# Expert weights of one decoder layer loaded as 2 MB units for a pair of experts, in nine buffers

## The chip, the cores and the metric

One core of one Trainium2 chip runs the whole program. The metric is the device time of one execution in microseconds (us); smaller is better. The engines are TensorE (PE in the profile: matrix products; PEld its weight loads), VectorE (DVE), ScalarE (ACT), GpSimd (POOL) and SyncE (SP), which issues most transfers. SBUF is the memory on the chip with 128 rows (partitions), PSUM the accumulators of TensorE. Transfers between HBM and SBUF run on 16 DMA engines.

## The reference, cut to what matters

One inference step of one decoder layer on 576 tokens (512 of a prompt, 64 of samples), model width 1024: a mixer (gated linear attention and dilated attention side by side), cross attention, and a mixture of experts; then a last norm. The change lies in the mixture of experts. Each token is sent to one of 4 groups and to 2 of the 8 experts in it, 32 experts in all. All arithmetic is in float32.

```python
def expert_block(a):
    xb, e = a
    return (jax.nn.silu(xb @ w_e1[e]) * (xb @ w_e3[e])) @ w_e2[e]
...
y = jax.ops.segment_sum(yb.astype(jnp.float32) * row_w[:, None], row_tok, num_segments=N + 1)[:N]
```

`w_e1` and `w_e3` are 1024 x 512 for each expert, `w_e2` is 512 x 1024: 6 MB an expert, 192 MB in all, each byte read once.

## The kernel before

Up to about 596 us the kernel computes the mixer, the cross attention and the routing. What follows is the expert loop at L1568, one turn for a **pair** of experts, p = 0 to 15; four pairs make one group of experts. Each expert has 64 places for tokens, so that a pair fills 128 rows.

One turn: `scales` (L1519, L1522) turns the routing weights of the pair. The **first products** at L1575 multiply the pair's tokens (tile `X`) by w_e1 and w_e3 (side by side, `w13`): for k = 0 to 7, column block c = 0, 1 (w_e1, w_e3) and expert e = 0, 1, each with 512 columns; the profile counts 64 instructions for a pair, since each float32 product is two. ScalarE's silu (L1597) and VectorE's product (L1600) make `sg`, four transposes follow (L1603), and the **second products** at L1616 multiply by w_e2 in two column blocks of 512 (32 instructions in the profile). `split_tile` (L243, L244) splits the result into two parts `yhi` and `ylo`, and `combine` (L1535 on TensorE, L1537 on VectorE) adds them to the rows of the group in `acc`. The combining of pair p runs in turn p + 1, half of it behind the first products, half behind the transposes. Where a group ends, `finish` norms its rows and stores them (L1367); meanwhile the next group's rows are fetched, split and gathered (`fetch_group`, `split_group`, `gather`, L1501 to L1509). In turn 9 `general` (L1448 on) looks on every engine whether some expert had more than 64 tokens; here none has, and the branch is not taken. In the last turn the second products go in four blocks of 256 columns, and `last_norm` (L1547 to L1558) norms the last rows behind them; POOL scales the first CUT = 128 columns there (L1556), ScalarE the next 384 (L1557), VectorE the rest (L1558).

**The weights.** `_lay_out` stores `w13` as 32 x 4 pieces and `w2` as 32 x 2 pieces, each 128 rows of 8 KB. One piece is one transfer of 1 MB, 12 for a pair (8 of w13, 4 of w2), 192 in all, each issued from SP by `load_one` (L1313 for w13, L1321 for w2). The last pair's w2 is the exception: its four 1 MB buffers hold one block of 256 columns of both experts, filled by two transfers each whose rows are in pieces of 1 KB (L1328). The buffers are a ring of 18 (`HOMES`): 13 in the pool `wpa`, which is there early, and 5 in `wpb`, whose space is free only when the routing is done. `loads_to` at the end of each turn lets the loads run 18 buffers ahead. What orders them on the chip: a transfer waits on SP for its buffer to be released by TensorE, and for its lane; SP has eight lanes for transfers, and so has at most eight in flight. Transfers 16 to 18 wait also for the first fetch of token rows (`i_first`, L1206), so that these come first. The rows of two groups lie in one tile `acc` of 128 x 4 x 1024 numbers, which the routing uses as scratch before.

Of the kernel before, what the change touches and what calls it, by code (L numbers as in the profile page):

```python
# [21 lines left out]
T = 576  # L22
NP_ = 512
D = 1024
# [3 lines left out]
CHUNK_A, CHUNK_B = 13, 5  # L28
PAY = 24
GENERAL = 9  # L30
CUT = 128
# [67 lines left out]
def _lay_out(inputs):  # L99
# [76 lines left out]
def body(ctx: ExitStack, tc: tile.TileContext, I, O, dbg=None):  # L176
# [847 lines left out]
    acc = keep.tile([128, 4, D], F32, name="acc")  # L1024
# [57 lines left out]
    with ExitStack() as st:  # L1082
        rp = pool(st, "route")
        space = acc.rearrange("p a c -> p (a c)")
        acc3, last = space[:, 0:T], space[:, T:2 * T]
        gp.memset(space[:, 2 * T:2048], 0.0)
        gp.memset(space[64:128, 3584:4096], 0.0)
        stage = [space[:, 2048 + i * 512:2560 + i * 512].rearrange("p (i c) -> p i c", c=128) for i in range(3)]
        stage4 = space[0:64, 3584:4096]
        hots = [space[:, a:a + 320].bitcast(BF16).rearrange("p (i c) -> p i c", c=128) for a in (2048, 3072)]  # L1090
# [115 lines left out]
        i_first = [fetch_rows(acc[:, t], src[:, t:t + 1]) for t in range(2)][-1]  # L1206
# [19 lines left out]
        posm = rt(5, 32)  # L1226
# [67 lines left out]
    def hp_():  # L1294
# [3 lines left out]
    HOMES = [(wpa, f"wa{i}") for i in range(CHUNK_A)] + [  # L1298
        (wpb, f"wb{i}") for i in range(CHUNK_B)]
# [3 lines left out]
    def wchunk():  # L1303
        home, tag = HOMES[len(ring) % RING]
        ring.append(home.tile([128, 2048], F32, name=f"wc{len(ring)}", tag=tag))
        return ring[-1]

    def load_one(p, n):

        w = wchunk()  # L1310
        if n < 8:
            q, h = divmod(n, 2)
            i_w = sy.dma_start(w, I["w13"][2 * p + h, q])  # L1313
            if CHUNK_A + 2 < len(ring) <= RING:
                tc.add_manual_dep(i_w.ins, i_first.ins.name, mybir.DependencyInfo(
                    mybir.DependencyClass.Sync, mybir.DependencyReason.DATA), reason="the first rows before more weights")
# [16 lines left out]
    def loads_to(n):  # L1333
        for i in range(len(ring), min(n, 192)):
            load_one(*divmod(i, 12))
# [228 lines left out]
    for p in range(16):  # L1564
        if p == 0:
            gather(0, oh, X, range(4))
# [77 lines left out]
```

## Time and profile before

| | us |
|---|---|
| median of three runs | 1080.32 (1078.32 to 1082.83) |
| profiled execution | 1076.97 |
| its span | 1075.3 |
| TensorE busy | 1019.0 (95%) |
| VectorE busy | 456.6 (42%) |
| ScalarE busy | 340.6 (32%) |
| POOL busy | 62.3 (6%) |

The span runs from the first to the last instruction of the profiled execution; the execution's own time has 1.67 us around it. Busy shares are means over the span: TensorE and the DMA engines are each full in different parts of it. The mean granted clock of TensorE was 0.978 of full speed. HBM reads were 290.30 MB.

### The profile page before, as it was taken

Reading aid. Unit: us, or ns where it says so; the run is one execution under the profiler, and the core shown is the slowest. Engines: PE = TensorE matmul, PEld = TensorE weight load, DVE = VectorE, ACT = ScalarE, POOL = GpSimd, SP = SyncE. Lnnn points to the kernel's source line nnn. Section 1 sums busy time; section 2 is a strip of 40 time slices with the busy share of each in tenths; the row PEclk is TensorE's granted clock in tenths of the full one; section 3 lists DMA queues with packets and bytes.
Section 4 is the critical chain, followed back from the end, with each engine's and each line's share of the span. In section 5 each row is a group of like instructions: output and inputs, shape, how many; then the busy total and the mean of one; then the engine's idle time right before and its main releaser. Section 6 shows DMA issues by size and latency. Waiting matters only on the chain. (4 is left out here: it accounts for less than half of the span.)

```text
span 1075.3 us, 17989 instructions
## 1 busy us (share of the span) xinstructions
PE 1019.0 (95%) x7375; PEld 711.8 (66%) x7375; DVE 456.6 (42%) x1043; ACT 340.6 (32%) x695; POOL 62.3 (6%) x87
## 2 busy tenths in 40 slices
PE   8999999999999999999997899999899969999996
PEld 7998889886779999888996444354435334443333
DVE  6337875357645764455333425223322322222113
ACT  5355323267444633333231111113211311122103
POOL 2100010000000200000111000001000100001002
PEclk9999999999999999999998799999999989999999
DMA  7312016517875752666693799999999999999993
GB/s 258 119 40 79 27 60 235 213 46 249 323 281 194 265 185 88 215 212 213 248 374 125 294 420 421 421 421 421 420 421 421 421 417 421 421 421 420 421 404 122
DMA packets 59674, 300.46 MB, mean 279 GB/s; under 512 B 7288, under 2 KB 13929, under 8 KB 35136
## 3 DMA queue, kind: packets, MB, share of 16 engines
q1 hardware_dynamic: 53856, 282.66, 67.7%
q0 software_dynamic: 5120, 16.28, 4.1%
q8 instruction: 59, 0.97, 0.4%
q10 hardware_dynamic: 608, 0.30, 0.1%
q14 instruction: 31, 0.25, 0.1%
HBM read 290.30 MB, written 12.19 MB: 281 GB/s over the span
## 5 line engine op out<-in xcount | busy, mean ns | idle before, releaser
L1575 PE MATMUL hp<-wc,X 128*64 128x512 f32 x1024 | 241.7, 595 | 6.3 <-DMA wc<-w 6.3
L1575 PEld LDWEIGHTS hp<-wc,X 128*64 128x64 f32 x1024 | 88.4, 137 | 151.5 <-issue 131.3
L283 PE MATMUL pj<-hi,whi 128*128 128x288 f32 (+1 forms) x544 | 163.0, 301 | 0.5 <-ACT R1t L193 0.5
L283 PE MATMUL pj<-hi,wlo 128*128 128x288 f32 (+1 forms) x544 | 162.4, 299 | 0.0
L283 PE MATMUL pj<-lo,whi 128*128 128x288 f32 (+1 forms) x544 | 162.1, 298 | 0.0
L1616 PE MATMUL hp<-wc,sg 128*64 128x512 f32 (+1 forms) x544 | 121.8, 575 | 0.1
L234 ACT ACTIVATE whi<-wst 128x1024 fp32r<-128x1024 f32 (+1 forms) x62 | 65.6, 1059 | 148.8 <-PE pj L283 121.1
L283 PEld LDWEIGHTS pj<-hi,whi 128*128 128x128 f32 x544 | 103.3, 190 | 4.2 <-issue 2.6
L283 PEld LDWEIGHTS pj<-hi,wlo 128*128 128x128 f32 x544 | 103.4, 190 | 1.7 <-issue 1.4
L283 PEld LDWEIGHTS pj<-lo,whi 128*128 128x128 f32 x544 | 103.4, 190 | 1.3 <-issue 0.8
L235 DVE TENSOR_TENSOR wlo<-wst,whi 128x1024 fp32r<-128x1024 f32 (+1 forms) x62 | 76.0, 1226 | 44.8 <-ACT whi L234 44.8
L1616 PEld LDWEIGHTS hp<-wc,sg 128*64 128x64 f32 x544 | 39.0, 138 | 69.9 <-issue 64.7
L1600 DVE SCALAR_TENSOR_TENSOR sg<-hp,sv,sg 128x512 f32<-128x512 f32 x16 | 12.0, 750 | 171.4 <-PE hp L1575 158.5
L1597 ACT ACTIVATE sg<-hp,sv 128x512 f32<-128x512 f32 x16 | 11.0, 687 | 195.7 <-PE hp L1575 195.7
L1537 DVE TENSOR_TENSOR acc<-acc,cp 128x512 f32<-128x512 f32 (+1 forms) x66 | 42.5, 667 | 61.7 <-PE cp L1535 61.2
L244 DVE TENSOR_TENSOR ylo<-hp,yhi 128x512 fp32r<-128x512 f32 (+1 forms) x34 | 22.4, 659 | 73.3 <-ACT yhi L243 71.4
L308 PE MATMUL pj<-whi,hi 128*128 128x256 f32 (+1 forms) x184 | 53.1, 288 | 0.0
L308 PE MATMUL pj<-wlo,hi 128*128 128x256 f32 (+1 forms) x184 | 52.8, 287 | 0.0
L308 PE MATMUL pj<-whi,lo 128*128 128x256 f32 (+1 forms) x184 | 52.5, 286 | 0.0
L243 ACT ACTIVATE yhi<-hp 128x512 fp32r<-128x512 f32 (+1 forms) x34 | 19.4, 571 | 83.8 <-PE hp L1616 82.0
L1501 PE MATMUL xp<-oh,pthi 128*128 128x256 f32 x128 | 34.7, 305 | 8.9 <-DVEq L1449 7.0
L283 PE MATMUL pj<-h1lo,whi 128*128 128x288 f32 x128 | 38.8, 303 | 0.0
(441 smaller groups left out, 1644.3 us busy)
## 6 DMA issues: line engine op xcount, KB each, us to landing
wc<-w SPq DMA_DIRECT2D x188, 1024.0 KB, 19.8
kv<-kc SPq DMA_DIRECT2D x16, 768.0 KB, 6.9
kv<-vc SPq DMA_DIRECT2D x16, 768.0 KB, 4.8
ckv<-mkc SPq DMA_DIRECT2D x16, 512.0 KB, 6.0
ckv<-mvc SPq DMA_DIRECT2D x16, 512.0 KB, 5.0
wst<-w_qkb SPq DMA_DIRECT2D x8, 512.0 KB, 3.6
wst<-w_mk SPq DMA_DIRECT2D x8, 512.0 KB, 5.6
wst<-w_mv SPq DMA_DIRECT2D x8, 512.0 KB, 4.5
```

Of the source, the lines that this page charges most:

```text
L234: ac.activation(hi[:, s], w[:, s], AF.Copy)
L235: ve.tensor_tensor(lo[:, s], w[:, s], hi[:, s].bitcast(F32), op=OP.subtract)
L243: ins = ac.activation(hi, x, AF.Copy)
L244: ve.tensor_tensor(lo, x, hi.bitcast(F32), op=OP.subtract)
L283: pe.matmul(p, lhsT=a[:, k], rhs=b[k][:, c], start=(k == 0 and s == 0), stop=(k == KT - 1 and s == 2))
L308: pe.matmul(outs[i][0:m], lhsT=a[xk][:, i * 128:i * 128 + m], rhs=b[:, k, :], start=(kh == 0 and k == 0 and s == 0 and head), stop=(kh == ...
L1501: pe.matmul(ps[:, k * 256:k * 256 + 256], lhsT=pt[s][:, c, kk * 128:kk * 128 + 128], rhs=oh[:, c], start=(k + c + s == 0), stop=(k + c + s ...
L1537: ve.tensor_tensor(a, a, ps, op=OP.add)
L1575: i_h = pe.matmul(H[c][rows[e]], lhsT=X[:, k, at + e * 64:at + e * 64 + 64], rhs=views[p, "in", k // 2, e](k % 2, c), start=(k == 0), stop ...
L1597: ac.activation(sg, H[0], AF.Silu, scale=sv[:, 0:1])
L1600: ve.scalar_tensor_tensor(sg, H[1], sv[:, 1:2], sg, op0=OP.mult, op1=OP.mult)
L1616: i_y = pe.matmul(Y[rows[e]], lhsT=hT_[:, j, rows[e]], rhs=views[p, "out", c, e](j), start=(j == 0), stop=(j == 3))
```

## The change

- **Layout.** `w13` and `w2` are stored by pair: a unit is 128 rows of 16 KB, of which the first 8 KB are the first expert's and the rest the second's. A unit is 2 MB and one transfer (L1329); a pair has six, four of w13 and two of w2, 96 in all.
- **Buffers.** The ring has nine homes of 2 MB instead of 18 of 1 MB, in the same space: six in `wpa`, one split home with a half in each pool, two in `wpb`. A unit in the split home comes as two transfers of 1 MB with 8 KB rows (L1332). With eight lanes up to 16 MB can now be in flight.
- **One-time buffers.** Pair 0's first unit goes not into the ring but into `w_first`, which lies in the second place of the rows' tile (not used until the second group's rows are fetched), and `wsecond`, which lies in one of the two places of `X`. `first_loads` issues these in an order of its own.
- **Rows.** `acc` becomes two turning tiles of 128 x 2 x 1024 (`group_rows`); the routing's scratch moves accordingly, and two memsets on POOL go.
- **The last pairs.** The loads end in the order w13 of pair 14, w13 of 15, w2 of 14, w2 of 15. The first products of pair 15 are issued ahead of the transposes and second products of pair 14. Pair 15's w2 has an array of its own, `w2l`: four transfers of 1 MB with 8 KB rows (L1335). The combining of pair 14 stands behind the first block of 256 columns of pair 15.
- **Last norm.** POOL's part of the scaling goes; ScalarE scales 512 columns.
- `general` and `dense`, for the case of too many tokens, read the new layout by pair and half.

```diff
-CHUNK_A, CHUNK_B = 13, 5
+UNITS_A, UNITS_B = 6, 2
...
-CUT = 128
...
-    w13 = np.concatenate([f["w_e1"][0], f["w_e3"][0]], 2).reshape(32, 4, 2, 128, 1024)
-    a["w13"] = ca(w13.transpose(0, 1, 3, 2, 4)).reshape(32, 4, 128, 2048)
-    w2 = f["w_e2"][0].reshape(32, 4, 128, 2, 512)
-    a["w2"] = ca(w2.transpose(0, 3, 2, 1, 4)).reshape(32, 2, 128, 2048)
+    w13 = np.concatenate([f["w_e1"][0], f["w_e3"][0]], 2).reshape(16, 2, 4, 2, 128, 1024)
+    a["w13"] = ca(w13.transpose(0, 2, 4, 1, 3, 5)).reshape(16, 4, 128, 4096)
+    w2 = f["w_e2"][0].reshape(16, 2, 4, 128, 2, 512)
+    a["w2"] = ca(w2.transpose(0, 4, 3, 1, 2, 5)).reshape(16, 2, 128, 4096)
+    a["w2l"] = ca(a["w2"][15].reshape(2, 128, 2, 4, 2, 256).transpose(0, 4, 1, 2, 3, 5)).reshape(4, 128, 2048)
...
-    acc = keep.tile([128, 4, D], F32, name="acc")
+    def group_rows():
+        return keep.tile([128, 2, D], F32, name="acc", bufs=2)
+    w_first = keep.tile([128, 2048], F32, name="wfirst", tag="acc", bufs=2)
+    accs = [group_rows()]
...
-    HOMES = [(wpa, f"wa{i}") for i in range(CHUNK_A)] + [
-        (wpb, f"wb{i}") for i in range(CHUNK_B)]
+    HOMES = [(wpa, f"wa{i}") for i in range(UNITS_A)] + [None] + [(wpb, f"wb{i}") for i in range(UNITS_B)]
     RING = len(HOMES)
     ring, views = [], {}
-    def wchunk():
-        home, tag = HOMES[len(ring) % RING]
-        ring.append(home.tile([128, 2048], F32, name=f"wc{len(ring)}", tag=tag))
+    def whome():
+        i = len(ring)
+        home = HOMES[i % RING]
+        if home:
+            w = home[0].tile([128, 4096], F32, name=f"wc{i}", tag=home[1])
+            ring.append([w[:, 0:2048], w[:, 2048:4096], w])
+        else:
+            ring.append([x.tile([128, 2048], F32, name=f"wh{i}", tag=t) for x, t in ((wpa, "wah"), (wpb, "wbh"))] + [None])
         return ring[-1]
-    def load_one(p, n):
-        w = wchunk()
-        if n < 8:
-            q, h = divmod(n, 2)
-            i_w = sy.dma_start(w, I["w13"][2 * p + h, q])
-            if CHUNK_A + 2 < len(ring) <= RING:
-                tc.add_manual_dep(i_w.ins, i_first.ins.name, mybir.DependencyInfo(
-                    mybir.DependencyClass.Sync, mybir.DependencyReason.DATA), reason="the first rows before more weights")
-            w = w.rearrange("p (k c) -> p k c", k=2)
-            views[p, "in", q, h] = lambda k2, c: w[:, k2, c * 512:c * 512 + 512]
-        elif p < 15:
-            c, h = divmod(n - 8, 2)
-            sy.dma_start(w, I["w2"][2 * p + h, c])
-            w = w.rearrange("p (j c) -> p j c", j=4)
-            views[p, "out", c, h] = lambda j: w[:, j]
+    order = [(p, n) for p in range(14) for n in range(6)] + [(p, n) for ns in (range(4), range(4, 6)) for p in (14, 15)
+                                                             for n in ns]
+    def load(i, w, halves=(0, 1)):
+        p, n = order[i]
+        if n < 4 or p < 15:
+            x = I["w13"][p, n] if n < 4 else I["w2"][p, n - 4]
+            if w[2] is not None:
+                out = sy.dma_start(w[2], x)
+            else:
+                for h in halves:
+                    out = sy.dma_start(w[h], x[:, h * 2048:h * 2048 + 2048])
         else:
-            c = n - 8
-            w = w.rearrange("p (h j c) -> p h j c", h=2, j=4)
             for h in range(2):
-                sy.dma_start(w[:, h], I["w2"][2 * p + h, c // 2].rearrange("p (j c) -> p j c", j=4)[
-                    :, :, c % 2 * 256:c % 2 * 256 + 256])
-            views[p, "out", c, 0] = lambda j: w[:, 0, j]
-            views[p, "out", c, 1] = lambda j: w[:, 1, j]
+                out = sy.dma_start(w[h], I["w2l"][2 * (n - 4) + h])
+        for h in range(2):
+            if n < 4:
+                views[p, "in", n, h] = lambda k2, c, v=w[h].rearrange("p (k c) -> p k c", k=2): v[:, k2, c * 512:c * 512 + 512]
+            elif p < 15:
+                views[p, "out", n - 4, h] = lambda j, v=w[h].rearrange("p (j c) -> p j c", j=4): v[:, j]
+            else:
+                for e in range(2):
+                    views[p, "out", 2 * (n - 4) + h, e] = lambda j, v=w[h].rearrange(
+                        "p (h j c) -> p h j c", h=2, j=4)[:, e]: v[:, j]
+        return out
+    loaded = [0]
     def loads_to(n):
-        for i in range(len(ring), min(n, 192)):
-            load_one(*divmod(i, 12))
+        n = min(n, len(order))
+        for i in range(loaded[0], n):
+            load(i, whome())
+        loaded[0] = max(loaded[0], n)
+    def first_loads():
+        first = [w_first, mw.tile([128, 2048], F32, name="wsecond", tag="X", bufs=2), None]
+        load(0, first, (0,))
+        for i in range(1, UNITS_A + 1):
+            load(i, whome())
+        split = whome()
+        load(UNITS_A + 1, split, (0,))
+        load(0, first, (1,))
+        load(UNITS_A + 1, split, (1,))
+        for i in range(UNITS_A + 2, RING + 1):
+            ins = load(i, whome())
+            tc.add_manual_dep(ins.ins, i_first.ins.name, mybir.DependencyInfo(
+                mybir.DependencyClass.Sync, mybir.DependencyReason.DATA), reason="the first rows before more weights")
+        loaded[0] = RING + 1
...
-            gp.tensor_scalar(a[:, 0:CUT], a[:, 0:CUT], r, None, op0=OP.mult)
-            ac.activation(a[:, CUT:512], a[:, CUT:512], AF.Copy, scale=r)
+            ac.activation(a[:, 0:512], a[:, 0:512], AF.Copy, scale=r)
...
+        sg = gated(p, H, sv)
+        if p == 14:
+            loads_to(len(order))
+            with tc.issue_after(i_h.ins):
+                so15 = scales(15, oh)
+                H15, i_h = first_products(15, X)
+        ps = turned(sg)
...
+    sv, oT = so15
+    sg = gated(15, H15, sv)
+    ps = turned(sg)
+    ac.activation(sg, ps, AF.Copy)
+    sgT = sg.rearrange("p (a b) -> p a b", a=4)
+    y = outputs(15)
+    for c in range(4):
+        i_y = second_products(15, c, 256, sgT, y)
+        with tc.issue_after(i_y.ins):
+            if c == 0:
+                combine(*done, slice(0, D))
+            elif c == 1:
+                combine(y, oT, 15, slice(0, 512), last_norm)
+            elif c == 3:
+                combine(y, oT, 15, slice(512, 768), last_norm)
+                combine(y, oT, 15, slice(768, D), last_norm)
```

How the instructions stand now, at three places. On SP, where the first weights are issued (wc are the ring's buffers, wst belongs to a projection ahead of the experts; the numbers count tiles), before:

```order
L1313 DMA wc_6719<-w 128x2048
L1313 DMA wc_6721<-w 128x2048
L1321 DMA wc_6723<-w 128x2048
L1321 DMA wc_6725<-w 128x2048
L1321 DMA wc_6727<-w 128x2048
L1321 DMA wc_6729<-w 128x2048
L1313 DMA wc_6731<-w 128x2048
L1313 DMA wc_6733<-w 128x2048
L1313 DMA wc_6735<-w 128x2048
L1313 DMA wc_6737<-w 128x2048
L1313 DMA wc_6739<-w 128x2048
L1313 DMA wc_6741<-w 128x2048
```

and after, where wfirst, wsecond and the halves wh of the split home stand among the ring's:

```order
L1332 DMA wfirst<-w 128x2048
L1329 DMA wc_6711<-w 128x4096
L229 DMA wst<-w_co 128x1024 x2
L1329 DMA wc_6713<-w 128x4096
L1329 DMA wc_6715<-w 128x4096
L1329 DMA wc_6717<-w 128x4096
L1329 DMA wc_6719<-w 128x4096
L1332 DMA wh_6721<-w 128x2048
L1332 DMA wh_6722<-w 128x2048
L1329 DMA wc_6726<-w 128x4096
L1332 DMA wsecond<-w 128x2048
L1329 DMA wc_6728<-w 128x4096
```

Before, 18 transfers of 1 MB are issued ahead of the first that waits for a release by the experts' products (wc_6963, the next of these on SP); the last three wait for the fetch of rows. After, wc_6709 (one wst ahead of wfirst) and these eleven, 20 MB in all, are; wc_6726 is the first that waits for the fetch, wsecond stands behind it, and wc_6951, the next on SP, waits for a release.

On TensorE, the end of the program, from the transposes of the last pair on, before:

```order
L1603 MATMUL xp<-ident,sg 128x128 x4
L1535 MATMUL cp<-yhi,oT 128x512
L1535 MATMUL cp<-ylo,oT 128x512
L1616 MATMUL hp<-wc_11188,sg 64x256
L1535 MATMUL cp<-yhi,oT 128x512
L1535 MATMUL cp<-ylo,oT 128x512
L1616 MATMUL hp<-wc_11188,sg 64x256 x7
L1616 MATMUL hp<-wc_11191,sg 64x256 x8
L1616 MATMUL hp<-wc_11194,sg 64x256
L1535 MATMUL cp<-yhi,oT 128x512 x2
L1535 MATMUL cp<-ylo,oT 128x512 x2
L1616 MATMUL hp<-wc_11194,sg 64x256 x7
```

and after, from the last two units of first products on:

```order
L1606 MATMUL hp<-wc_12003,X 64x512 x8
L1606 MATMUL hp<-wc_12005,X 64x512 x8
L1622 MATMUL xp<-ident,sg 128x128 x4
L1635 MATMUL hp<-wc_12007,sg 64x512 x8
L1635 MATMUL hp<-wc_12072,sg 64x512 x8
L1635 MATMUL hp<-wc_12074,sg 64x256 x8
L1570 MATMUL cp<-yhi,oT 128x512
L1570 MATMUL cp<-ylo,oT 128x512
L1570 MATMUL cp<-yhi,oT 128x512
L1570 MATMUL cp<-ylo,oT 128x512
L1635 MATMUL hp<-wc_12074,sg 64x256 x3
L1570 MATMUL cp<-yhi,oT 128x512
```

Before, the four blocks of pair 15 follow its own first products. After, its first products (wc_12005 is their last unit) stand ahead of pair 14's second products (wc_12007 and wc_12072), and its own blocks (wc_12074, and behind these rows wc_12077) come last; the combining of pair 14 (L1570) stands between its first two blocks.

On SP, the last weights, before:

```order
L1313 DMA wc_11087<-w 128x2048
L1313 DMA wc_11089<-w 128x2048
L1313 DMA wc_11184<-w 128x2048
L1313 DMA wc_11186<-w 128x2048
L1328 DMA wc_11188<-w 128x4x256 x2
L1328 DMA wc_11191<-w 128x4x256 x2
L1328 DMA wc_11194<-w 128x4x256 x2
L1328 DMA wc_11197<-w 128x4x256 x2
```

and after:

```order
L1329 DMA wc_12001<-w 128x4096
L1329 DMA wc_12003<-w 128x4096
L1329 DMA wc_12005<-w 128x4096
L1329 DMA wc_12007<-w 128x4096
L1329 DMA wc_12072<-w 128x4096
L1335 DMA wc_12074<-w2l 128x2048 x2
L1335 DMA wc_12077<-w2l 128x2048 x2
```

The eight transfers of 1 KB pieces (128x4x256) become four of whole rows from `w2l`, and the last w13 unit moves ahead of the w2 of pair 14.

## Rows read from the trace of the kernel before

**Rows 1.** the page's busy tenths in 40 slices of the span, and GB/s

```profile
PE   8999999999999999999997899999899969999996
DMA  7312016517875752666693799999999999999993
GB/s 258 119 40 79 27 60 235 213 46 249 323 281 194 265 185 88 215 212 213 248 374 125 294 420 421 421 421 421 420 421 421 421 417 421 421 421 420 421 404 122
```

**Rows 2.** the chain of waits, its longest pieces: start, us, what

```profile
907.15 19.81 DMA wc<-w
...
1027.70 19.95 DMA wc<-w
1047.69 3.65 PE hp L1575 x12
```

**Rows 3.** the waits: engine and line, for what: us, times, longest

```profile
SPq L1313 <- DMA wc<-w: 183.4, 87, 3.4
...
PEld hp L1575 <- DMA wc<-w: 17.2, 20, 2.2
```

**Rows 4.** windows: length, busy by engine (count), PEclk, DMA share, GB/s

```profile
272.00:280.00 8.00, 8.00 (x116) 5.99 (x104) 4.41 (x12) 3.80 (x9) 0.00 (x0) 1.00 1.02 421
464.00:468.00 4.00, 3.88 (x21) 3.13 (x20) 1.78 (x4) 1.34 (x5) 0.00 (x0) 1.00 1.01 412
640.00:860.00 220.00, 214.56 (x1050) 95.50 (x1048) 64.51 (x148) 44.69 (x87) 7.40 (x7) 0.99 1.01 421
884.00:1040.00 156.00, 151.60 (x710) 66.37 (x709) 35.99 (x67) 29.34 (x56) 2.82 (x2) 1.00 1.01 421
1045.00:1050.00 5.00, 4.34 (x17) 1.45 (x16) 0.00 (x0) 0.00 (x0) 0.00 (x0) 1.00 0.99 331
```

**Rows 5.** DMA issues of the page whose rows are 6 and 4 KB

```profile
kv<-kc SPq DMA_DIRECT2D x16, 768.0 KB, 6.9
...
ckv<-mkc SPq DMA_DIRECT2D x16, 512.0 KB, 6.0
```

**Rows 6.** windows at the start of the expert loop

```profile
606.00:608.00 2.00, 2.00 (x12) 0.98 (x12) 0.32 (x2) 0.61 (x2) 0.00 (x0) 1.00 0.06 20
608.00:610.00 2.00, 2.00 (x12) 0.72 (x10) 0.00 (x0) 0.00 (x0) 0.00 (x0) 1.00 0.00 0
610.00:612.00 2.00, 2.00 (x12) 0.70 (x10) 0.00 (x0) 0.00 (x0) 0.00 (x0) 1.00 0.93 266
```

**Rows 7.** timeline of SP at the start: start, us, line, operation

```profile
596.47 1.28 SPq L1313 DMA_DIRECT2D wc<-w  x3
609.08 1.17 SPq L1313 DMA_DIRECT2D wc<-w  x2
```

**Rows 8.** timeline of PE in pair 0

```profile
607.10 13.09 PE L1575 MATMUL hp<-wc,X 128*64 128x512 f32 x58
624.88 7.09 PE L1616 MATMUL hp<-wc,sg 128*64 128x512 f32 x32
631.79 13.90 PE L1575 MATMUL hp<-wc,X 128*64 128x512 f32 x64
```

**Rows 9.** windows at the end of the stream

```profile
1055.00:1060.00 5.00, 4.53 (x36) 2.66 (x34) 1.50 (x4) 0.77 (x2) 0.00 (x0) 1.00 0.29 98
1058.00:1059.00 1.00, 0.53 (x7) 0.08 (x3) 0.03 (x1) 0.38 (x1) 0.00 (x0) 1.00 0.03 11
```

**Rows 10.** timeline of PE and POOL at the end

```profile
1054.85 3.67 PE L1616 MATMUL hp<-wc,sg 128*64 128x256 f32 x32
1058.99 0.73 PE L1535 MATMUL cp<-yhi,oT 128*128 128x512 f32 x2 [0.47 <-ACT yhi L243]
1060.12 3.67 PE L1616 MATMUL hp<-wc,sg 128*64 128x256 f32 x30
1067.53 1.89 POOL L1556 TENSOR_SCALAR acc<-acc,tail_s 128x128 f32<-128x128 f32 x2 [3.51 <-ACT tail_s L1555]
1069.59 1.04 POOL L1367 DMA_INDIRECT o_y<-acc,dst  x1 [0.17 <-POOL acc L1556]
```

More of the change, by code (lines that the diff above doesn't have):

```diff
@@ L1083, in body @@
         rp = pool(st, "route")
[L1084 to L1090, printed above, removed]
+        space = accs[0].rearrange("p a c -> p (a c)")
+        acc3, last = rpool.tile([128, T], F32, name="R1"), rp.tile([128, T], F32, name="last")
+        stage = [space[:, i * 512:i * 512 + 512].rearrange("p (i c) -> p i c", c=128) for i in range(3)]
+        stage4 = space[0:64, 1536:2048]
+        hots = [x[:, 0:320].bitcast(BF16).rearrange("p (i c) -> p i c", c=128) for x in (acc3, last)]
         idb = rp.tile([128, 5, 2], BF16, name="idb")
@@ L1205, in body @@
         ve.tensor_copy(src[:, 0:2], f)
-        i_first = [fetch_rows(acc[:, t], src[:, t:t + 1]) for t in range(2)][-1]
+        i_first = [fetch_rows(accs[0][:, t], src[:, t:t + 1]) for t in range(2)][-1]
         late_ = ExitStack()
@@ L1398, in features, with dense @@
                                  op0=OP.mult)
[L1400 removed]
+    def dense(Xe, sv, pair, h, add):
         def piece(x):
             w = mw.tile([128, 512], F32, name="piece", tag="sq")
[L1403 removed]
+            gp.dma_start(w, x.rearrange("n p c -> p (n c)"))
             return w
@@ L1562, in body, with first_products @@
     split_group(0)
-    so, done, nxt = None, None, None
-    for p in range(16):
-        if p == 0:
-            gather(0, oh, X, range(4))
-        if p % 4 == 0 and p != GENERAL - 1 or p % 4 == 3 and p < 15:
-            nxt = slots_of(p // 2 + 1), tokens_x()
-        so = scales(p, oh)
+    def first_products(p, X):
         H = [hp_(), hp_()]
@@ L1576, in body, with gated, turned, outputs @@
                                     rhs=views[p, "in", k // 2, e](k % 2, c), start=(k == 0), stop=(k == KT - 1))
+        return H, i_h
+    def gated(p, H, sv):
+        sg = mw.tile([128, 512], F32, name="sg", tag="sq" if p == 15 else "sg")
+        ac.activation(sg, H[0], AF.Silu, scale=sv[:, 0:1])
+        if p == 15:
+            tc.keep_in_program_order(ac.preload_act_table_set("natural_log_exp_and_others"))
+        ve.scalar_tensor_tensor(sg, H[1], sv[:, 1:2], sg, op0=OP.mult, op1=OP.mult)
+        return sg
+    def turned(sg):
+        ps = xp_()
+        for j in range(4):
+            pe.transpose(ps[:, j * 128:j * 128 + 128], sg[:, j * 128:j * 128 + 128], ident)
+        return ps
+    def outputs(p):
+        if p == 15:
+            return [mw.tile([128, 2, D], F32R, name=name)[:, 0] for name in ("pthi", "ptlo")]
+        return [mw.tile([128, D], F32R, name=name) for name in ("yhi", "ylo")]
+    def second_products(p, c, w, sgT, y):
+        cs = slice(c * w, c * w + w)
+        Y = hp_()[:, 0:w]
+        for j in range(4):
+            for e in range(2):
+                i_y = pe.matmul(Y[rows[e]], lhsT=sgT[:, j, rows[e]], rhs=views[p, "out", c, e](j), start=(j == 0),
+                                stop=(j == 3))
+        split_tile(Y, *(z[:, cs] for z in y))
+        return i_y
+    done, nxt = None, None
+    for p in range(15):
+        if p == 0:
+            gather(0, oh, X, range(4))
+        if p % 4 == 0 and p != GENERAL - 1 or p % 4 == 3:
+            nxt = slots_of(p // 2 + 1), tokens_x()
+        so = scales(p, oh)
+        H, i_h = first_products(p, X)
         sv, oT = so
@@ L1579, in body @@
             if done:
-                combine(*done, slice(0, D if p == GENERAL else 512))
+                combine(*done, slice(0, D if p in (GENERAL, 14) else 512))
             if p == 0:
```

75 lines of the change are left out of this document (29 added, 46 removed).

## The prediction

> **What bounds the kernel now.** I read the page's slices first, then the chain of waits, then the waits and windows of the stretch the chain names. The slices [rows 1] show two regimes. Until about slice 22 TensorE is full while the DMA engines are half empty; from slice 23 on the DMA engines are full too and move 420 to 421 GB/s in nearly every slice. The chain [rows 2] says which of the two decides: from 907 us to 1047.69 it runs through weight transfers alone, one after the other, each some 19.8 us from issue to landing: eight times the 2.49 us that 1 MB takes at 421 GB/s, as eight of 1 MB are in flight. TensorE then follows the last first-product chunk. SP, which issues the weights, waits 183.4 us in 87 steps for an earlier transfer to land [rows 3], so the queue of transfers is never empty; TensorE's own waits for weights are short, 17.2 us over the whole loop [rows 3], since its time per pair is only a little under the DMA's. So from the first release of a weight buffer on, the end is set by: the time the stream starts, its bytes by its rate, and what follows its last bytes. I cost each of these three.
>
> The profiled execution took 1076.97 us, its span 1075.3; the 1.67 us around the span stay. The median of three is 1080.32, 3.35 above the profiled execution; I make the sum on the profiled one and carry the difference over.
>
> **Start of the stream.** Before, the last three of 18 MB are held until the first token rows have come; SP issues them at 596.47 [rows 7]. The DMA engines have run dry by 606, stand at zero in 608 to 610, and move again from about 610.7 (266 GB/s over 610 to 612) [rows 6]: 1.6 us after 609.08, where the first buffer is free again [rows 7]. At that point 192 − 18 = 174 MB are left. After, pair 0's first unit lies in two one-time buffers, so 20 MB go before the first release, 5 MB of them after 596.47. Two megabytes more take 2 × 2.491 = 4.98 us at 421 GB/s. But the first buffer that comes free is now a whole unit of 2 MB, and it is the unit behind the one-time buffers: it is done after 32 first products and not after the first few. First products run from 607.10 at 13.09/58 = 0.226 us each [rows 8]; six of the 64 are done by then, so 26 more end at 613.0. The half unit `wsecond` stands behind a 2 MB transfer at the gate (3 MB after 596.47: 1.6 + 7.5 us and a late last engine, 606 to 609) and TensorE wants it at 607.10; I add 1.0. The release is then at 614.0, the first bytes at 615.6, 4.9 later, with 172 MB left instead of 174: 4.9 − 4.98 = **−0.1**. A second, small hole comes with the second products of pair 0 (from 624.88, 7.09 us for 32 [rows 8]): the three units freed by the first products last 15 us, until 630.5; the first unit of second products is free after 16 of them, at 624.88 + 1.0 + 3.5, bytes 1.6 later, 631.0 to 631.4. I take **+1.0**, ends 0 and +1.5. From pair 1 on (631.79) TensorE frees 2 MB in 3.5 us and the DMA needs 5, so there is no third hole.
>
> **Rate.** Units of 2 MB have rows of 16 KB instead of 8. The rate of the stream by size of row can be read in this trace: 331 GB/s while the last pair's 1 KB rows move, 412 for the 4 KB rows of ckv, 421 for the 6 KB rows of kv, 421 for 8 KB rows in two long windows [rows 4, 5]. One engine's time for a row is 16 × bytes / rate: 159.1 ns at 4 KB and 311.3 ns at 8 KB. The line through these two has 0.0372 ns per byte and 6.9 ns per row; 16 KB gives 615.7 ns, 425.8 GB/s, 2.463 us per MB instead of 2.491. That line puts 6 KB rows at 418 and they show 421, so the fixed part may be smaller still, down to none (421, no gain). The line through 1 KB (49.5 ns) and 8 KB has 12.1 ns per row and gives 429.3 GB/s, 2.442. I take the one through 4 and 8 KB, since its points are nearest. Of 172 MB, 18 go into the split home (8 KB rows) and 4 are the last pair's; 150 MB × −0.028 = **−4.2**, ends 0 and −7.3.
>
> The Trainium skill ("DMA: Bandwidth & Descriptors", section "Rules for kernel authors") asks for 128 partitions and at least 1 MiB per DMA for the most bandwidth, which the transfers of before already have: by that rule the rate term is nothing, and the sum 1077.3. The trace does not decide between the two; it has no row over 8 KB.
>
> **Last pair's second weights.** 4 MB in rows of 1 KB at 331 GB/s take 3.168 us per MB [rows 4]; from the new array they come in 8 KB rows at 2.491: 4 × −0.677 = **−2.7**.
>
> **Tail behind the stream.** Before, the DMA engines are on average done at 1055 + 0.29 × 5 = 1056.45 [rows 9], and 18.85 us remain. After, the first products of pair 15 stand ahead, and the last 4 MB are those of pair 15's second products. The last unit of pair 14 so lands 9.97 us ahead of the stream's mean end, plus the lag of the slowest engine. For that lag: the last bytes before come 2 us behind the mean end [rows 9], and the last chunk of first products was there at 1047.69 [rows 2] where 4 MB × 3.168 ahead of 1056.45 is 1043.8, a lag of 3.9. I take 3. TensorE then has 16 products of 512 columns at 7.09/32 (3.55 us), 64 of 256 columns at 3.67/32 (7.34), and 12 combining products at 1.13/4 (3.4) [rows 8, 10]: 14.3 us. From the end of the second products (1063.79) before, 11.5 us remain to the end; of these POOL's two scalings of 128 columns (1067.53, 1.89 us, the first store at 1069.59 right behind them [rows 10]) are gone. ScalarE's longer copy and VectorE's half end at about 1068.3, so the stores move by 1.2: 10.3. Sum: −9.97 + 3 + 14.3 + 10.3 = 17.6, against 18.85: **−1.2**; ends −4.2 (no lag) and −0.3 (3.9).
>
> **What I cost at nothing.** The wait for the route scratch in its new home ends before the gate. The longer queue of waits on SP stands behind nothing but weights. The general path, with TensorE idle for 7 us after pair 9, keeps its place, and the stream runs through it. The bytes of token rows and stores in the stream do not change. If TensorE became the bound, faster weights would bring nothing more, but it would have to be some 15 us later.
>
> **Sum**: −0.1 + 1.0 − 4.2 − 2.7 − 1.2 = −7.2. Profiled 1076.97 − 7.2 = 1069.8; median 1080.32 − 7.2 = **1073.1**.
>
> **Rivals.**
> 1. The rate stays at 421. For it: 6 KB and 8 KB rows show the same rate, as if 421 were a ceiling. Against: 4 KB rows at 412 are still on a slope. The sum loses 4.2: −3.0, **1077.3**.
> 2. The start is later. If the transfers at the gate share the engines, `wsecond` comes with all 5 MB, at 596.47 + 1.6 + 12.5 = 610.6. TensorE then stands 3.5 us instead of 1, and everything behind the first release moves by 2.5: **1075.6**, with the unchanged rate 1079.8. Against: eight transfers in flight land one by one in the chain [rows 2], not together.
> 3. Slower than before: 16 KB rows move more slowly than 8 KB ones, since the 16 engines now read from places 128 KB apart instead of 64, and each row fills one partition twice as long. The other terms give −3.0, so the time of before is reached where 150 MB cost 0.020 us per MB more, at 417.6 GB/s. At the 412 GB/s that the 4 KB rows show it is +8.2 − 3.0: **1085.5**. For it speaks nothing in the trace but that no row over 8 KB is in it; against it, that every longer row so far was as fast or faster.
> 4. The change does not do what it says, where a row of 16 KB is moved as two packets of 8 KB: then the page counts as many packets as before, and the time is rival 1's.
>
> **Chances and range.** The forecast 0.48, with 424 to 430 GB/s and the start as worked out; the rate unchanged (rivals 1 and 4) 0.26; the later start 0.14; slower rows 0.12. A measurement of this kernel can tell about 0.5%, 5.4 us, from no change: faster is below 1074.9, slower above 1085.7. The forecast's own range is 1068 (429 GB/s and no lag in the tail would be 1067) to 1075. For 8 in 10 it has to take in the unchanged rate, with the late start 1079.8; below 1067 and above 1080 I leave 2 in 10. Faster 0.55: nearly all of the forecast and a part of the later start. Slower 0.10. The same 0.35.
>
> **What would show it.** Start: first release near 614, DMA at zero from about 611 to 615, second hole near 631 of about 1 us. Rate: a window from 640 to 860 above 424 GB/s, with half as many packets; at 421 the rate term is wrong. Last pair: no stretch at 331 GB/s. Tail: 17 to 18 us from the DMA engines' mean end to the span's end, no POOL scaling ahead of the stores. The whole is wrong if the chain runs through TensorE in pairs 10 to 15 and not through weights.

## The result, and the profile after

The changed kernel takes 1086.8 us (median of 8, 1086.13 to 1090.7) against 1080.56 (median of 8, 1077.84 to 1082.83): a ratio of 1.0069, with a 95% interval of 1.0054 to 1.0085. It is slower by some 0.7%, where I had forecast 1073.1. The profiled execution took 1089.22 us, its span 1087.5; it is 12.3 us over the profiled one of before, twice what the medians differ by, so the traces show the loss larger than it mostly is.

The page after, its slices of TensorE, of the DMA engines and of the bytes, to be held against [rows 1]:

```profile
PE   8999999899999999999997899999399976999996
DMA  7312116526885752666693799999999998999991
GB/s 255 118 39 78 29 57 233 209 58 235 318 307 180 245 175 88 206 212 216 254 373 119 283 408 428 424 430 425 426 416 425 428 424 338 428 425 427 428 424 59
```

The rate is what I forecast, 424 to 430 GB/s in nearly every slice of the stream where 420 to 421 stood. But TensorE has a new hole (the 3 in slice 28, counted from 0), and the one that was there before (the 6 in slice 32) is wider (the 7 and 6 in 32 and 33); behind it the stream itself falls to 338. The windows after, over the two stretches of [rows 4], say the same: 425 in the first, 412 in the second.

```profile
640.00:860.00 220.00, 202.51 (x1001) 88.06 (x998) 57.91 (x137) 37.61 (x72) 4.87 (x4) 0.96 1.01 425
884.00:1040.00 156.00, 137.56 (x679) 64.63 (x678) 37.82 (x69) 29.99 (x56) 4.87 (x4) 0.93 0.98 412
```

The chain after no longer runs through weights, as it did in [rows 2]. The page's shares of the span by engine:

```profile
issue 24%; PE 15%; DMA 4%; POOL 1%; ACT 0%; DVE 0%; POOLq 0%; DVEq 0%
```

and its three longest transfers (start, us, what):

```profile
750.20 15.00 DMA o_y<-acc,dst
...
872.78 13.59 DMA o_y<-acc,dst
887.23 19.21 DMA acc<-rows_d,src
```

The 24% of "issue" are mostly three stretches of 37, 109 and 102 us on POOL's queue, between its transfers, which the chain puts down to no releaser. So ahead of 907 us the chain only points at POOL's transfers; that they cost time is for the experiments to show. The transfers in it are the stores of finished token rows (`o_y`) and the fetches of the next rows (`acc<-rows_d`), both issued by POOL. My prediction had no line for how long these take. Here they are on POOL's timeline, before, around pair 5 (start, length of the issue, line, and in brackets what ended the wait):

```profile
739.97 1.81 POOL L1367 DMA_INDIRECT o_y<-acc,dst  x1 [109.48 <-DVE acc L1387]
742.09 0.99 POOL L1367 DMA_INDIRECT o_y<-acc,dst  x1 [0.30 <-issue]
749.88 1.04 POOL L1061 DMA_INDIRECT acc<-rows_d,src  x1 [6.79 <-DMA o_y<-acc,dst]
753.29 1.01 POOL L1061 DMA_INDIRECT acc<-rows_d,src  x1 [2.37 <-ACT sg L1597]
```

and after:

```profile
748.09 1.81 POOL L1401 DMA_INDIRECT o_y<-acc,dst  x1 [109.55 <-DVE acc L1421]
750.20 1.00 POOL L1401 DMA_INDIRECT o_y<-acc,dst  x1 [0.30 <-issue]
766.00 1.05 POOL L1068 DMA_INDIRECT acc<-rows_d,src  x1 [14.80 <-DMA o_y<-acc,dst]
767.35 1.01 POOL L1068 DMA_INDIRECT acc<-rows_d,src  x1 [0.31 <-issue]
```

Before, the first fetch goes 9.9 us behind its store. After, both fetches go only when the second store is through, 15.8 us behind it. What waits for the fetch: ScalarE's splitting of the next group's rows (`pthi`) stands in its queue in pair 5, two pairs ahead of the pair that needs it, and ahead of the copies of gathered tokens (`X`) that TensorE wants at once. TensorE's wait there, before and after, and ScalarE's behind the fetch after:

```profile
762.46 0.83 PE L1519 MATMUL xp<-pay,oh 128*128 128x3 f32 x4 [4.65 <-ACT X L1507]
```

```profile
781.97 0.63 ACT L245 ACTIVATE pthi<-acc 128x512 fp32r<-128x512 f32 x1 [20.60 <-DMA acc<-rows_d,src]
```

```profile
783.38 1.01 PE L1554 MATMUL xp<-pay,oh 128*128 128x3 f32 x4 [17.46 <-ACT X L1542]
```

In pair 9 there is a second one. TensorE's wait for the branch of the general path was there before, 7.0 us long. Behind it stands a new one: the first copies of `X` there, VectorE's at 906.74 and ScalarE's at 906.68, come just after the last fetch (issued at 888.57) is through. Here the split does not stand ahead of them in ScalarE's queue (`pthi` follows at 911.04); the copy itself is shown as waiting for the fetch. On TensorE:

```profile
894.40 0.55 PE L1536 MATMUL xp<-oh,pthi 128*128 128x256 f32 x1 [7.53 <-DVEq L1484]
...
907.67 0.58 PE L1536 MATMUL xp<-oh,pthi 128*128 128x256 f32 x1 [9.52 <-DVE X L1544]
...
912.45 0.61 PE L1554 MATMUL xp<-pay,oh 128*128 128x3 f32 x4 [0.89 <-ACT X L1542]
```

and on ScalarE:

```profile
906.68 0.84 ACT L1542 ACTIVATE X<-xp,gmoe 128x256 f32<-128x256 f32 x2 [10.98 <-DMA acc<-rows_d,src]
```

Each of the two waits costs a little more than its length: TensorE's granted clock, full ahead of them, is at its lower level (0.50, 1.2 GHz) for 17 and 20 us around them. Windows after (the seventh entry is the clock, the second TensorE's busy time):

```profile
766.00:770.60 4.60, 0.00 (x0) 0.00 (x0) 0.33 (x1) 0.00 (x0) 2.06 (x2) 1.00 0.97 411
770.60:787.70 17.10, 4.32 (x14) 2.14 (x16) 2.90 (x6) 3.78 (x8) 0.00 (x0) 0.50 1.02 429
...
890.00:910.60 20.60, 6.68 (x29) 6.41 (x30) 2.35 (x5) 2.81 (x4) 0.00 (x0) 0.50 1.01 422
```

What this costs is an estimate: the four products of L1554 behind a wait take 1.01 us at the lower level (783.38) and 0.61 at the full one (912.45), so the 4.32 and 6.68 us of work at the lower level would have taken some 6.6 us at the full one. The 4 to 5 us are a part of the loss, and not all of them are new: before, too, the clock fell there, but for less long (4.2 us at 0.59 in pair 5).

```profile
762.00:766.20 4.20, 3.74 (x12) 1.72 (x14) 2.29 (x6) 2.83 (x7) 0.00 (x0) 0.59 1.04 431
```

### The profile page after: what moved, and what is told of

Its sections match the earlier page's. It is cut to its first block, busy times and chain, and to the rows that moved or that the text cites. A ratio compares the mean times of both kernels' runs of the same rounds, so it can differ in the third digit from the quotient of the medians.

```text
span 1087.5 us, 17808 instructions
## 1 busy us (share of the span) xinstructions
PE 1011.6 (93%) x7375; PEld 708.7 (65%) x7375; DVE 456.9 (42%) x1043; ACT 341.0 (31%) x695; POOL 58.4 (5%) x83
## 3 DMA queue, kind: packets, MB, share of 16 engines
q1 hardware_dynamic: 38256, 282.66, 66.0%
## 5 line engine op out<-in xcount | busy, mean ns | idle before, releaser
L1606 PE MATMUL hp<-wc,X 128*64 128x512 f32 x912 | 203.7, 592 | 0.0
L1606 PEld LDWEIGHTS hp<-wc,X 128*64 128x64 f32 x912 | 70.1, 137 | 126.3 <-issue 123.4
L1635 PE MATMUL hp<-wc,sg 128*64 128x512 f32 (+1 forms) x480 | 103.1, 567 | 0.1
L1635 PEld LDWEIGHTS hp<-wc,sg 128*64 128x64 f32 x480 | 34.1, 137 | 59.3 <-issue 56.4
L1536 PE MATMUL xp<-oh,pthi 128*128 128x256 f32 x128 | 36.1, 313 | 18.7 <-DVE X L1544 9.5
L246 DVE TENSOR_TENSOR ylo<-hp,yhi 128x512 fp32r<-128x512 f32 x30 | 20.7, 691 | 72.0 <-ACT yhi L245 72.0
L245 ACT ACTIVATE yhi<-hp 128x512 fp32r<-128x512 f32 x30 | 17.9, 597 | 77.5 <-PE hp L1635 75.8
L1536 PEld LDWEIGHTS xp<-oh,pthi 128*128 128x128 f32 x128 | 27.4, 214 | 21.9 <-DVE X L1544 9.8
## 6 DMA issues: line engine op xcount, KB each, us to landing
wc<-w SPq DMA_DIRECT2D x83, 2048.0 KB, 19.2
```

What stands on the lines that cost most here:

```text
L245: ins = ac.activation(hi, x, AF.Copy)
L246: ve.tensor_tensor(lo, x, hi.bitcast(F32), op=OP.subtract)
L1536: pe.matmul(ps[:, k * 256:k * 256 + 256], lhsT=pt[s][:, c, kk * 128:kk * 128 + 128], rhs=oh[:, c], start=(k + c + s == 0), stop=(k + c + s ...
L1606: i_h = pe.matmul(H[c][rows[e]], lhsT=X[:, k, at + e * 64:at + e * 64 + 64], rhs=views[p, "in", k // 2, e](k % 2, c), start=(k == 0), stop ...
L1635: i_y = pe.matmul(Y[rows[e]], lhsT=sgT[:, j, rows[e]], rhs=views[p, "out", c, e](j), start=(j == 0), stop=(j == 3))
```

## The experiments

Theory P: a store or fetch of token rows shares each DMA engine with the weights packet by packet, so that the length of the weights' packets sets how long it takes; TensorE waits for that. Rivals: F, the 16 MB in flight; S, the start of the stream and what is ahead of it. To read the pairs I took, from TensorE's instructions in the trace, the time from the last second product of pair 4 to that of pair 5 ("pair 5" below): 32.37 us before, 45.57 after.

**8 KB rows in the changed kernel.**

```diff
-                out = sy.dma_start(w[2], x)
+                both[:] = [sy.dma_start(w[h], x[:, h * 2048:h * 2048 + 2048]) for h in range(2)]
+                out = both[1]
```

> The changed kernel with each 2 MB unit issued as two transfers of 1 MB with 8 KB rows (first and second expert's half), both into the same buffer; layout, buffers, order and tail as changed. Theory P (packets): a store or fetch of token rows shares each DMA engine with the weights row by row, so 16 KB rows lengthen it, and TensorE waits for that in pairs 5 and 9. Then here the stores land after some 9.6 us again instead of 12.4 (median) and the fetches after 8.5 instead of 12.0, the gap in pair 5 falls from 17.5 us to some 8 to 10, the stream is at 421 GB/s and the bound again, and the time is that of before less the terms that stay: about 1077.5 us (1075 to 1080). Theory F (16 MB in flight instead of 8 make the queue that a row transfer stands in): the same here, 8 MB are in flight. Theory S (the time is lost ahead of and at the start of the stream, by the new placement and the 2 MB releases; the row transfers don't matter): as changed or a little above, 1086 to 1091.

Measured: 1079.6 us, ratio 1.0012 (0.9994 to 1.0031). With rows of 8 KB the loss is gone, and the stream is the bound again at 421 GB/s. The transfers are also smaller and less is allowed in flight, so P and F stand; S falls. Pair 5 takes 37.37 us, still 5.0 more than before; TensorE's wait there is 8.02 us instead of 4.65:

```profile
766.50 1.01 PE L1558 MATMUL xp<-pay,oh 128*128 128x3 f32 x4 [8.02 <-ACT X L1546]
```

**16 KB rows in half transfers.** The aim was 16 KB rows with 8 MB in flight.

```diff
-                out = sy.dma_start(w[2], x)
+                both[:] = [sy.dma_start(w[2][h * 64:h * 64 + 64], x[h * 64:h * 64 + 64]) for h in range(2)]
+                out = both[1]
```

> The changed kernel with each 2 MB unit issued as two transfers of 1 MB, each of 64 partitions with 16 KB rows: 8 MB in flight as before the change, rows as after it. Theory P: stores and fetches stay at 12 us (median) and the gap in pair 5 near 17 us; time as changed, 1085 to 1091. Theory F: stores 9.6 and fetches 8.5 us, gap 8 to 10, and with 425 GB/s the time falls to 1073 to 1078. Theory S: as changed, with row transfers either way.

Measured: 1469.19 us (four runs, 1395.67 to 1485.76). It doesn't tell P from F, as something else happened: transfers to 64 partitions run at half the rate. The window of 640 to 860:

```profile
640.00:860.00 220.00, 152.47 (x628) 61.11 (x626) 41.67 (x124) 26.25 (x51) 5.88 (x5) 0.85 1.01 222
```

and the row of the stores among the DMA issues (the last number is the median from issue to landing, in us):

```profile
o_y<-acc,dst POOLq DMA_INDIRECT x8, 18.7
```

The engines are as busy as ever (share 1.01) at 222 GB/s, so each 16 KB row took 16 x 16384 / 222 = 1181 ns instead of 616, and the stores took 18.7 us instead of 12.4. These transfers are of 1 MB, as those with 8 KB rows are, so the stores don't follow the size of the transfers.

**8 MB in flight, whole transfers.** Each unit also waits on SP for the unit four ahead of it to land.

```diff
+        sent.append(out)
+        if len(sent) > 8 and sent[-5] is not None:
+            tc.add_manual_dep(out.ins, sent[-5].ins.name, mybir.DependencyInfo(
+                mybir.DependencyClass.Sync, mybir.DependencyReason.DATA), reason="four units in flight")
```

> The changed kernel where each weight unit also waits until the unit four before it has landed: 16 KB rows as changed, but 8 MB in flight as in the kernel before. Theory P (a row transfer takes turns with the weights packet by packet on each engine, so the length of a packet counts): stores and fetches as changed, 12.4 and 12.0 us median, the gap in pair 5 near 17 us, 1085 to 1090 us. Theory F (the queue of 16 MB counts): 9.6 and 8.5 us, gap 8 to 10, 1073 to 1079 us.

Measured: 1086.52 us, ratio 1.0072 (1.0048 to 1.0095); pair 5 47.20 us. Stores and fetches as in the changed kernel. But the changed kernel did not have 16 MB in flight here either: its units of 2 MB take 19.2 us from issue to landing (median), which at 425 GB/s is some 8 MB (an estimate over the whole loop). In this run they take 18.5. The changed kernel and this run:

```profile
wc<-w SPq DMA_DIRECT2D x83, 2048.0 KB, 19.2
```

```profile
wc<-w SPq DMA_DIRECT2D x83, 2048.0 KB, 18.5
```

With 8 KB rows the 1 MB transfers take 19.8 us, again some 8 MB (eight of them), and the stores 9.6 us. So with about the same amount in flight the stores differ with the rows, and F, which needs more in flight to explain them, falls; that more in flight adds nothing is seen in the late split below.

**4 KB rows.** Each unit in four transfers of 512 KB.

```diff
-                out = sy.dma_start(w[2], x)
+                both[:] = [sy.dma_start(w[2][:, h * 1024:h * 1024 + 1024], x[:, h * 1024:h * 1024 + 1024]) for h in range(4)]
+                out = both[-1]
```

> The changed kernel with each 2 MB unit issued as four transfers of 512 KB with 4 KB rows. Theory P: the stores and fetches are faster than with 8 KB rows (9.6 and 9.2 us median there, 12.4 and 12.0 with 16 KB): 6 to 8 us, and pair 5 takes 31 to 35 us instead of 37.4. The stream is slower, about 412 GB/s as other 4 KB rows of this kernel, so the time is above that of the 8 KB rows (1079.6): 1083 to 1092. If row transfers have a floor apart from the weights' packets, they stay at 9 us.

Measured: 1092.16 us, ratio 1.0117 (1.0095 to 1.0139), at 410 GB/s; pair 5 28.48 us, less than before the change and less than I had put down. The row transfers got faster and the stream slower, both as P says; the stores (8.2 us) stay just above the 6 to 8 that I expected. The fetches and stores of four kernels (DMA issues, median from issue to landing), in the order 4 KB rows, 8 KB rows, changed, changed with 8 MB in flight:

```profile
acc<-rows_d,src POOLq DMA_INDIRECT x8, 7.8
o_y<-acc,dst POOLq DMA_INDIRECT x8, 8.2
```

```profile
acc<-rows_d,src POOLq DMA_INDIRECT x8, 9.2
o_y<-acc,dst POOLq DMA_INDIRECT x8, 9.6
```

```profile
acc<-rows_d,src POOLq DMA_INDIRECT x8, 12.0
o_y<-acc,dst POOLq DMA_INDIRECT x8, 12.4
```

```profile
acc<-rows_d,src POOLq DMA_INDIRECT x8, 11.9
o_y<-acc,dst POOLq DMA_INDIRECT x8, 12.3
```

One weight row of 4, 8 and 16 KB takes an engine 159, 311 and 616 ns (16 x bytes / rate), and in the half transfers 1181. The stores take 8.2, 9.6, 12.4 and 18.7 us. From each to the next the store grows by 9 to 11 times what the packet grows: (9.6 − 8.2)/0.152 = 9.2, 2.8/0.305 = 9.2, 6.3/0.565 = 11.2. Spread evenly over 16 engines, the 128 rows of a store are 8 for each, so by this estimate a row waits for about one weight packet, or a little more (1.2 to 1.4). This agrees with the Trainium skill ("DMA: Bandwidth & Descriptors", section "SWDGE vs HWDGE vs iDMA"), by which an engine goes round-robin between its internal queues, one of them fed by POOL's transfers and another by SP's.

**The whole-group tile alone.** In the kernel before, a fetch also waits for both stores of the group whose place it takes, as the tile of a whole group makes it do.

```diff
-            fetch_rows(acc[:, t % 4], src[:, t:t + 1], True)
+            i_f = fetch_rows(acc[:, t % 4], src[:, t:t + 1], True)
+            for i_s in stored_rows.get(g - 2, []):
+                tc.add_manual_dep(i_f.ins, i_s.name, mybir.DependencyInfo(
+                    mybir.DependencyClass.Sync, mybir.DependencyReason.DATA), reason="both stores")
```

> The kernel before, in which the fetch of a token tile also waits for both stores of the group whose place it takes, as the changed kernel's tile of a whole group makes it do, and not only for its own; weights in 8 KB rows. If the whole-group tile is the part of the loss that remains with 8 KB rows (pair 5, from one end of second products to the next, took 32.4 us before, 37.4 in the changed kernel with 8 KB rows, 45.6 in the changed kernel), pair 5 takes 36 to 38 us here; since the stream bounds this kernel the time stays within 2 us of 1078.6. If the fetch's place in a tile doesn't matter, pair 5 stays at 32 to 33.

Measured: 1079.03 us, ratio 0.9999 (0.9981 to 1.0016); pair 5 37.34 us. So the 13.2 us that pair 5 lost are 5.0 for the tile (32.37 to 37.34, and 37.37 in the changed kernel with 8 KB rows) and 8.2 for the 16 KB rows (37.37 to 45.57). The kernel before can bear the 5.0 without a loss of time, as it is bound by the stream.

**No stores.** The changed kernel without the norm and stores of the first three groups; that part of the output is left out.

```diff
-        if p % 4 == 0 and p:
+        if False:
             g = p // 4 - 1
             finish([(accs[g][:, t % 2], dst[:, t:t + 1]) for t in (2 * g, 2 * g + 1)], True)
```

> The changed kernel without the norm and the stores of the first three groups' rows (that part of the output is left out; the fetches stay). If the wait of pair 5 is the chain of store, fetch and split, taking the store away lets the fetch go some 15 us earlier: the gap in pair 5 falls from 17.5 us to under 4, the one behind the general path from some 10 us to none, and the time to 1072 to 1077 us. If the fetch alone or the start makes the loss, 1083 us or more.

Measured: 1070.25 us, ratio 0.9922 (0.9898 to 0.9945); pair 5 26.02 us, and no wait behind the general path. That is below the 1072 that I had as the lower end; some of the gain is the left-out work and bytes themselves.

**Late split.** The weights stay as changed. The split of the next group's rows is queued behind the pair ahead of the one that needs it, and the last fetch comes behind the general path.

```diff
-            if p % 4 == 1 and 4 < p < 12:
+            if p in (5, GENERAL + 1):
                 fetch_group(p // 4 + 1)
             if p % 4 == 3:
-                split_group(p // 4 + 1)
+                with tc.issue_after(last_copy.ins), tc.issue_after(last_gate.ins):
+                    split_group(p // 4 + 1)
```

> The changed kernel with the splitting of the next group's rows on ScalarE and VectorE queued behind the pair before the one that needs them (behind pair 2, 6 and 10 instead of into pairs 1, 5 and 9), and the last group's fetch moved behind the general path (from pair 9 to pair 10). Weights untouched. Theories P and F: stores and fetches still take 12 to 15 us, but nothing waits for them; the gap of 17.5 us in pair 5 and that of some 10 us behind the general path are gone, the stream never runs dry behind them, and with 425 GB/s the time is 1073 to 1078. Theory S: 1085 to 1090, since the start is as changed.

Measured: 1073.74 us, ratio 0.9955 (0.994 to 0.997). Stores and fetches take as long as in the changed kernel (12.3 and 11.7 us), pair 5 25.93 us, and the loss has become a gain. More is in flight here, as the units take 30.5 us from issue to landing, some 13 MB at 426 GB/s, and the stores are no slower for it:

```profile
wc<-w SPq DMA_DIRECT2D x83, 2048.0 KB, 30.5
```

The page's bytes by slice no longer fall anywhere in the stream:

```profile
GB/s 258 120 40 79 40 47 236 211 42 256 324 263 197 261 200 79 207 208 212 252 363 164 255 380 427 425 428 427 424 428 425 426 423 427 426 427 425 426 426 122
```

and the window of 640 to 860 has TensorE at 214.53 us of work again, at the faster rate:

```profile
640.00:860.00 220.00, 214.53 (x1060) 91.84 (x1058) 63.95 (x140) 45.08 (x87) 7.69 (x6) 1.00 1.01 426
```

The same two edits in the kernel before:

> The kernel before with the same two edits: split queued behind pairs 2, 6 and 10, last fetch in pair 10. All theories: before is bound by the stream at 421 GB/s, which the 8 us gap in pair 5 did not touch, so 1080.5 us, within 2; a gain of over 4 us would say that TensorE's waits bounded the kernel before as well.

Measured: 1078.75 us, ratio 1.0008 (0.9991 to 1.0024), though pair 5 fell from 32.37 to 25.97. Before, the wait was under the stream; it was there and cost nothing.

**Late split, early fetch.** The same, but the last fetch stays in pair 9 (`if p in (5, GENERAL)`).

> The changed kernel with the late split (behind pairs 2, 6 and 10) but the last group's fetch left in pair 9 ahead of the general path. Pair 5's wait (19.6 us over the 25.9 that the pair takes without one) goes, the wait of some 10 us behind the general path in pair 9 stays. If both waits count, the time lies between the late split with the late fetch (1073.7) and the changed kernel (1086.8): TensorE is then late by some 5 us in pair 9, which the stream's own lateness can cover or not: 1074 to 1079.

Measured: 1073.81 us, ratio 0.9949 (0.993 to 0.9969), no different from the late fetch. The wait behind the general path is 2.81 us here instead of 9.52: TensorE, no longer late from pair 5, has to wait for weights in pair 9 and comes to the general path later after the stores, and the fetch has more time. So the second wait of the changed kernel follows from the first, in the main. What is left of it is not the split's, which is queued behind pair 10 here: ScalarE's first copy of `X` still starts only when the fetch is through.

```profile
885.57 0.84 ACT L1542 ACTIVATE X<-xp,gmoe 128x256 f32<-128x256 f32 x2 [4.57 <-DMA acc<-rows_d,src]
```


**First unit in the ring.** Late split, and the one-time buffers hold pair 0's second unit.

```diff
-        load(0, first, (0,))
-        for i in range(1, UNITS_A + 1):
+        load(0, whome())
+        load(1, first, (0,))
+        for i in range(2, UNITS_A + 1):
             load(i, whome())
         split = whome()
         load(UNITS_A + 1, split, (0,))
-        load(0, first, (1,))
+        load(1, first, (1,))
```

> The late-split kernel (1073.7 us) with the one-time buffers holding pair 0's second unit instead of its first: the unit that TensorE uses first is then a ring buffer and free after 16 instead of 32 first products. The stream, which starts again at about 618 us there and stands for 5 us before, should start 3.5 us earlier with the same 20 MB loaded, and if the stream bounds that kernel the time falls by about 3, to 1070 to 1072 us; if TensorE's own chain bounds it by then, less than 1 us.

Measured: 1072.56 us, ratio 0.9943 (0.9922 to 0.9963), not to be told from the late split (1073.74), so neither the 3 us that I expected nor their absence is shown. The stream did restart earlier, at about 613.0 instead of 618.7, but stands again in two places. Windows (DMA share second to last):

```profile
612.00:614.00 2.00, 2.00 (x12) 0.66 (x10) 0.00 (x0) 0.00 (x0) 0.00 (x0) 1.00 0.78 213
618.00:620.00 2.00, 2.00 (x12) 0.67 (x10) 0.00 (x0) 0.00 (x0) 0.00 (x0) 1.00 0.76 180
630.00:632.00 2.00, 2.00 (x12) 0.71 (x10) 0.69 (x1) 0.53 (x1) 1.48 (x2) 1.00 0.65 139
```

## Why the prediction was wrong

**The step that failed is "What I cost at nothing".** It said that the bytes of token rows and stores don't change, and that TensorE would have to be some 15 us later to become the bound. The first is true and beside the point: not their bytes but their time from issue to landing changed, by 2.8 us for the median store and 3.5 for the median fetch, and in pair 5 by more for those that come last (the second store took 10.14 us before and 15.00 after, the second fetch 7.66 and 14.51). TensorE stands behind a chain of a store, a fetch and a split. The change lengthened this chain in two ways, and I named neither. The rows of a group became one tile, which I passed over with "the route scratch in its new home". The other is the 16 KB rows themselves; of the 13.2 us that pair 5 lost, 5.0 are the tile's and 8.2 the rows'. And TensorE did become late: against before, pair 5 lost 13.2 us and pair 9 another 6.5 (43.46 to 50.00), on top of the 8 by which its last second product of pair 4 was late (747.17 against 739.02; most of these 8 are the start of this execution, see what stays open). The "some 15 us" had no working behind it, but the size was about right: TensorE ends pair 9 26.7 us late (920.35 against 893.67) and the second products of pair 15 13.0 us late (1076.78 against 1063.79). What was wrong is that I saw nothing in the change that makes it so late. In the kernel before, the wait showed as 4.65 us of TensorE in pair 5, and the page's row of the stores stood at 9.6 us; I read [rows 3] for weights alone.

My condition "the whole is wrong if the chain runs through TensorE in pairs 10 to 15" is what happened: the chain after runs through its products from 907.67 on.

**The rest of the sum, seen where nothing waits.** With the late split the kernel is bound by the stream, and the steps of the sum can be read there. It gives 1073.74, close to the 1073.1 of the sum, but that is luck: the kernel before has 1078.49 in the same set of runs, so the gain is 4.75 us and not 7.2. The profiled executions differ by 2.6 (1074.35 against 1076.97): start +8.0, stretch of the stream −12.0, tail +1.3.

*Rate*: 426 GB/s over 640 to 860 (425 in the changed kernel), where the line through 4 and 8 KB gave 425.8. Right. Rival 1 (the rate stays at 421) and rival 4 are wrong, and so, for the rows here, is what I read out of the Trainium skill ("DMA: Bandwidth & Descriptors", section "Rules for kernel authors"), that transfers of 1 MB have nothing to gain: the windows have 425 and 426 against 421. The changed kernel's page counts 38256 packets on SP's queue, the 8 KB rows 50208. Rival 3 (16 KB rows are slower) falls with the same windows.

*Start*: with the late split the units at the gate go at 599.35 instead of 596.47, and the stream restarts at about 618.7 instead of 610.7. I had 4.9 us of these 8.0; 2.9 are the later gate. From the gate to the first bytes it is 19.3 us, where I had 19.1 (596.47 to 615.6), so the 2.5 us of rival 2 are not there. The second hole is there and a little smaller than I had it (634 to 636 at a share of 0.66, so 0.7 us instead of 1.0):

```profile
614.00:618.00 4.00, 4.00 (x22) 1.52 (x20) 0.00 (x0) 0.00 (x0) 0.00 (x0) 1.00 0.00 0
618.00:620.00 2.00, 2.00 (x12) 0.79 (x9) 0.00 (x0) 0.00 (x0) 0.00 (x0) 1.00 1.02 279
...
634.00:636.00 2.00, 2.00 (x12) 0.63 (x10) 0.00 (x0) 0.27 (x1) 0.15 (x1) 1.00 0.66 231
```

*Tail*: wrong. I had 17.6 us from the engines' mean end to the end of the span; it is 20.1. The windows at the end:

```profile
1050.00:1055.00 5.00, 5.00 (x32) 2.80 (x30) 2.80 (x5) 0.97 (x2) 0.00 (x0) 1.00 0.48 200
1055.00:1060.00 5.00, 4.53 (x34) 2.53 (x36) 2.50 (x5) 1.72 (x5) 0.63 (x1) 1.00 0.01 5
```

and the piece of the chain in which TensorE takes up the last unit of pair 14:

```profile
1046.29 5.38 PE hp L1635 x32
```

The mean end is 1050 + 0.48 x 5 + 0.05 = 1052.45, the span's 1072.6. The last unit of pair 14 is used at 1046.29, 6.2 us ahead of the mean end (I had 7.0), the products from there to 1061.87 take 15.6 us (I had 14.3), and 10.7 remain (I had 10.3): three small errors of one sign, 2.5 together, which make of my gain of 1.2 a loss of 1.3.

*Last pair's weights*: no stretch at 331 GB/s is left. The whole stretch from the first byte to the mean end is 433.8 us with the late split and 445.8 before; the four terms in it (2 MB fewer to load, 16 KB rows, 8 KB rows for the last pair, the second hole) summed to −10.9, measured −12.0.

**What stays open.** In the profiled execution of the changed kernel the gate is at 603.71, 7.2 us later than before. In seven runs of its variants (all but the half transfers) it is at 597.65 to 602.22, 599.3 on average, and in the kernel before and its two variants at 595.48 to 597.08. So more than half of the 7.2 belongs to this execution, but some 3 us seem to be the change's, and my sum had none. What makes them I have not tried to find. It also stays open why the first copies of `X` behind the general path wait for the fetch.

## What to carry to other kernels

A stream whose rows are made longer can make every small transfer beside it later, here by about one packet of the stream for each row that the small one has on an engine: ask who waits for the small ones, and read their time from issue to landing as closely as that of the large ones. A wait of TensorE that costs nothing under a stream that bounds the kernel is a debt that falls due when the stream gets faster, so look for such waits first, and move the work that waits (here the split, two pairs too early in ScalarE's queue) to where it is needed. Before two small buffers are joined into one tile, see what frees each of them.

## What the runs showed that I had not expected

Transfers of 1 MB to 64 partitions with 16 KB rows ran at 222 GB/s with all engines busy, against 425 for 2 MB to 128 partitions with the same rows. The same stream gives 410 GB/s with rows of 4 KB, 421 with 8 and 425 to 426 with 16: the 4 to 5 GB/s from 8 to 16 KB are a little under half of what 4 to 8 KB bring, and still there. With 128 partitions a longer row is also a larger transfer (512 KB, 1 MB, 2 MB); no run here separates the two.
